# A two-layer transformer trunk on one core: loads of summed tiles issued six tiles back, two rests behind the shared results

## The chip, the core and the metric

The kernel runs on one core of a Trainium2 chip. What is measured is the device time of one execution in microseconds (us). Three runs of the kernel before gave 2206.82, 2209.60 and 2212.26 us; their median is 2209.6.

A core has five engines that run their own instruction queues and meet at semaphores: PE (TensorE, matrix products into the PSUM banks), DVE (VectorE, elementwise work), ACT (ScalarE), POOL (GpSimd, here only issuing transfers) and SP (SyncE, here only issuing transfers). Each engine takes its instructions strictly in order. Transfers from memory, whoever issues them, are carried by 16 DMA engines.

## The reference

`S` = 256 tokens of width 2048 go through two layers, everything in float32:

```python
for l in range(DEPTH):
    h = rms_norm(x, pre_mix_norm[l])
    m = hybrid_mixer(h, l, ...)          # w_in, two kinds of attention, w_o
    x = x + rms_norm(m, post_mix_norm[l])
    h = rms_norm(x, pre_ffn_norm[l])
    f = (silu(h @ w_gate[l]) * (h @ w_up[l])) @ w_down[l]
    x = x + rms_norm(f, post_ffn_norm[l])
```

`w_gate` and `w_up` are 2048 x 5632, `w_down` is 5632 x 2048. The weights are most of the 457 MB that are read in a run.

## The kernel before

**Weights as a stream.** The weights lie in memory as one list of tiles in the order of use, `weights_in_turn`: tile i has 128 partitions of 2 x 512 numbers, 512 KB, and holds two blocks of 128 rows by 512 columns of one matrix. In the texts "raw162" is tile 162 of this stream.

**Split products.** For float32 accuracy each operand is split into a high part and a rest. For a weight tile, ACT copies `raw` to `hi` (a shorter format, L271) and DVE subtracts it, `lo = raw - hi` (L273, called the "rest"). PE then makes three products per block: high by high, high by rest, rest by high (`product`, L976 to L978). The buffers: 4 of `raw`, 6 of `hi`, 6 of `lo`. A `raw` buffer is free for the next load when its rest has been made.

**Seven products in place of eight.** In the feed-forward part some pairs of tiles (`sevens`) are used in a form that needs seven block products where eight would stand, in the manner of Strassen and Winograd. Such a pair is a G tile (the gate tile, or the first of two down tiles) and a T tile (its partner). T is loaded by SP (L223), and then a second transfer, issued by POOL, adds one half of the G tile's data from memory onto its first half (`accum_op=ALU.add`, L224). `mixed_weights` makes the other sums of the pair on DVE and splits them: `hi`/`lo` from T, `Th`/`Tl` from further sums. In chunk 0 of the gate and up products two of eight pairs are such pairs, in chunk 1 three, in the others four; in each half of the down product seven of 22.

**Shared results.** Four of the seven products land in four PSUM banks of their own (`p1`, `p6`, `p7`, `q5`), over all pairs of a chunk. After the chunk's last such pair, `shared_part` turns them into four tiles `w[0]` to `w[3]`: one copy on ACT, four sums on DVE, at L1014 to L1017. They are then added to the chunk's other four banks (L1152, L1154). The banks are used in turn by the next chunk, which cannot begin in a bank before it has been read.

**The order of work.** `weights(i, ahead)` calls `feed(i + 1 + LOOKAHEAD)`, and that calls `fetch`, so loads and splits of a tile are written four tiles before its products. `fetch` also loads T tiles up to `EARLY` = 4 tiles beyond: it writes the load of a T before the load of the tile it is looking at. A scheduler then sets each engine's order, moving loads ahead as buffers come free. There are three G buffers and four T buffers in the gate and up products, and three of each in the down product. Behind the front, for instance, SP's order in layer 0 is raw161, T169, G164, T171, G168, T173, raw162; DVE's is L1014, a rest, L1015, L1016, L1017, a rest.

**The stages of a layer.** The input projection and attention, the output projection, then the gate and up products in 11 chunks of 512 columns (layer 0 from about 405 us, layer 1 from about 1500 us), then the down product in two halves, with a tail of three pairs at the end of the second.

Of the kernel before, what the change touches and what calls it, by code (L numbers as in the profile page):

```python
# [2 lines left out]

# [6 lines left out]
F32 = mybir.dt.float32  # L10
# [3 lines left out]
ALU = mybir.AluOpType  # L14
# [7 lines left out]
NT = S // P  # L22
# [27 lines left out]
WARM = 13  # L50
LEVEL = 232
EARLY = 4
X_BACK = 12


# [4 lines left out]
def gate_sevens(c):  # L60

    return (FIRST_SEVEN, NEXT_SEVEN)[c] if c < 2 else SEVEN
# [89 lines left out]
def kernel(  # L152
# [15 lines left out]
    nc = tc.nc  # L168
# [14 lines left out]
    def four_banks(odd, names):  # L183
        makers = (bank, bank, bank, last_bank) if odd else (acc_bank,) * 4
        return [make(n) for make, n in zip(makers, names)]
# [3 lines left out]
    stream = [weights_in_turn[i].rearrange("p (k n) -> p k n", k=2) for i in range(len(order))]  # L189

    ready = {}
    raws, loads = [], []
    fed = [0]

    def fetch(upto):
        while len(raws) < min(upto, len(stream)):
            i = len(raws)
            for j in range(i, min(i + EARLY + 1, mix_raw[3])):
                if j in sevens and j not in sums:
                    summed(j)  # L200
            if i in sevens:
                raws.append(sums[i])
                continue
            if i + 1 in sevens:
                g = mix_raw[0].tile([P, 2, CW], F32, tag="G", bufs=mix_raw[1], name=f"G{i}")
                loads.append(nc.sync.dma_start(g, stream[i]))
                raws.append(g)
                continue
            if i in own or i + 1 in own:
                raw = mix_pool[0].tile([P, 2, CW], F32, tag="v", bufs=2, name=f"V{i}")  # L210
            elif i in plain or i + 1 in plain:
                raw = mix_pool[0].tile([P, 2, CW], F32, tag="GU", bufs=4, name=f"GU{i}")
            else:
                raw = wpool.tile([P, 2, CW], F32, tag="raw", bufs=4, name=f"raw{i}")
            loads.append(nc.sync.dma_start(raw, stream[i]))
            raws.append(raw)

    sums = {}

    def summed(i):  # L220

        sums[i] = mix_raw[0].tile([P, 2, CW], F32, tag="T", bufs=mix_raw[2], name=f"T{i}")
        loads.append(nc.sync.dma_start(sums[i], stream[i]))  # L223
        nc.gpsimd.dma_start(sums[i][:, 0, :], stream[i - 1][:, 0, :], accum_op=ALU.add)  # L224

    mix_pool = [None]
# [34 lines left out]
    def feed(upto):  # L261
        fetch(upto)
        while fed[0] < min(upto, len(stream)):
            i = fed[0]
            raw = raws[i]
            if i in sevens or i in plain or i in own:
                ready[i] = mixed_weights(i)
                fed[0] += 1
                continue
            hi = wpool.tile([P, 2, CW], F32R, tag="hi", bufs=6, name=f"hi{i}")  # L270
            nc.scalar.activation(hi, raw, AF.Copy)  # L271
            lo = wpool.tile([P, 2, CW], F32R, tag="lo", bufs=6, name=f"lo{i}")
            rest = nc.vector.tensor_tensor(out=lo, in0=raw, in1=hi.bitcast(F32), op=ALU.subtract)  # L273
            ready[i] = (hi, lo)
            fed[0] += 1
            rests.append(rest)

    rests = []

    def after_rests():  # L280

        return tc.issue_after(rests[-1].ins)
# [5 lines left out]
    def weights(i, ahead):  # L288
        feed(i + 1 + ahead)
        return ready[i]  # L290
# [175 lines left out]
    def start(gen, n=1):  # L466
        running.append([clock[0] + n, gen])
# [542 lines left out]
    def shared_part(extra, w):  # L1010

        p1, p6, p7, q5 = extra
        nc.scalar.copy(w[0], p1)
        nc.vector.tensor_tensor(out=w[1], in0=p6, in1=w[0], op=ALU.subtract)  # L1014
        nc.vector.tensor_tensor(out=w[2], in0=p7, in1=w[1], op=ALU.add)  # L1015
        nc.vector.tensor_tensor(out=w[1], in0=q5, in1=w[1], op=ALU.add)  # L1016
        nc.vector.tensor_tensor(out=w[3], in0=q5, in1=w[2], op=ALU.add)  # L1017

    def shared_sign(t, col):
        return ALU.subtract if (t, col) == (1, 0) else ALU.add  # L1020

    xT = None
    for l in range(L):
# [11 lines left out]
        mg = {}  # L1035
# [16 lines left out]
        for kp in LATE_O:  # L1052
            i, j = (plan[l]["o"][c, kp] for c in (2, 3))
# [4 lines left out]
            if kp == O_SEVEN[0]:  # L1058
                extra = four_banks(False, [f"{q}_o{l}" for q in ("p1", "p6", "p7", "q5")])
            hi, lo = weights(i, LOOKAHEAD)  # L1060
# [64 lines left out]
        for c in range(FF // CW):  # L1125
            banks = four_banks(1 - c % 2, [f"c{q}_{l}_{c}" for q in ("11", "12", "21", "22")])
            mine = gate_sevens(c)
            order = FIRST_ORDER if c == 0 else tuple(range(KT // 2))
            if c == 0:
                for t in range(NT):  # L1130
                    for kp in order[:2]:
                        eight(banks, c, kp, (t,), kp == order[0], False)
                order = order[2:]
            extra = None
            for n, kp in enumerate(order):
                if (c, n) in FORM_AT:
                    with after_rests():
                        pair_sums(FORM_AT[c, n])
                if kp not in mine:
                    eight(banks, c, kp, range(NT), kp == 0, kp == order[-1])  # L1140
                    continue
                if kp == mine[0]:
                    extra = four_banks(c % 2, [f"{q}_{l}_{c}" for q in ("p1", "p6", "p7", "q5")])
                seven(banks, extra, c, kp, kp == mine[0], kp == mine[-1])
                if kp == mine[-1]:
                    w = [pool.tile([P, CW], F32, tag="t2", name=f"w{j}_{l}_{c}") for j in range(4)]
                    shared_part(extra, w)
            at = pool.tile([P, 4, S], F32, tag="act", bufs=FF // CW, name=f"act{l}_{c}")
            act.append(at)
            sg = [w[0], w[2]]  # L1150
            for t, u in ((0, w[1]), (1, w[3])):
                nc.vector.tensor_tensor(out=sg[t], in0=banks[2 * t], in1=sg[t], op=shared_sign(t, 0))  # L1152
                nc.scalar.activation(sg[t], sg[t], AF.Silu, scale=rs[t][:, 0:1])
                nc.vector.tensor_tensor(out=u, in0=banks[2 * t + 1], in1=u, op=ALU.add)  # L1154
                nc.vector.scalar_tensor_tensor(out=sg[t], in0=u, scalar=rs[t][:, 0:1], in1=sg[t], op0=ALU.mult, op1=ALU.mult)

            def flip(sg=sg, at=at, c=c):
                for t in range(NT):
                    pb = (acc_bank if c % 2 else bank)(f"actT_ps{l}_{c}_{t}")
                    for j in range(4):  # L1160
                        nc.tensor.transpose(pb[:, j * P : (j + 1) * P], sg[t][:, j * P : (j + 1) * P], ident)
                    nc.scalar.copy(at[:, :, t * P : (t + 1) * P], pb.rearrange("p (k q) -> p k q", k=4))
                    yield 1

            start(flip(), DEFER_ACT)
# [7 lines left out]
        mg = {}  # L1173
        ssm = [small.tile([P, 4], F32, tag="ssm", name=f"ssm_d{l}_{t}") for t in range(NT)]
        nkp = FF // P // 2
        for half in range(2):
# [48 lines left out]
            for kp in range(nkp - tail):  # L1225
                if half == 1 and kp == X_BACK:
                    back = [pool.tile([P, 4, S], F32, tag="act", bufs=FF // CW, name=f"xd{l}_{n}") for n in range(4)]
                    back = [b.rearrange("p k n -> p (k n)") for b in back]
                    xs[:] = [back[:2], back[2:]]
                    with in_turn():  # L1230
                        for t, h in ((0, 0), (0, 1), (1, 0), (1, 1)):
                            load_x(t, h, away[-1])
                if kp not in mine:
                    down(kp, range(NT))
                    continue
                if kp == mine[0]:
                    extra = four_banks(1 - half, [f"{q}_d{l}_{half}" for q in ("p1", "p6", "p7", "q5")])
                down_seven(kp)
                if kp == mine[-1]:
                    for t in range(NT):  # L1240
                        mg[t, half] = dn.tile([P, 2, CW], F32, tag="qk", bufs=4, name=f"mg_d{l}_{t}_{half}")
                    shared_part(extra, [mg[t, half][:, j, :] for t in range(NT) for j in range(2)])
                    if open_sums[0]:
                        for c in cc:
                            nc.vector.tensor_tensor(out=accs[c, 1], in0=accs[c, 1], in1=mg[1, half][:, c % 2, :], op=shared_sign(1, c % 2))
# [5 lines left out]
            for t in range(NT):  # L1251
# [4 lines left out]
                for c in cc:  # L1256
                    for kp in range(nkp - tail, nkp):
# [3 lines left out]
                        hi, lo = weights(plan[l]["down"][c, kp], LOOKAHEAD)  # L1261
# [67 lines left out]
```

## Time and profile before

| | |
|---|---|
| median of three runs | 2209.6 us (2206.82 to 2212.26) |
| the profiled execution | 2204.91 us |
| its span in the profile | 2203.2 us |
| clock granted to PE | 0.999 |
| PE / DVE / ACT / POOL busy | 2180.6 / 1902.2 / 1371.9 / 140.2 us |
| DMA, mean | 212 GB/s |
| loads from SP of ordinary, T and G tiles | 522, 110 and 110, of 512 KB each |
| sums onto T tiles, issued by POOL | 110, of 256 KB each |

How to read it: a busy row gives an engine's busy time, its share of the span and its instructions. PEld is the loading of weights into PE's array, which overlaps the products. A row of a timeline gives the start, the duration, the engine, the line and operation, and in brackets how long the engine stood idle before and what released it. A row such as "lo<-raw,hi" names what is written and what is read. SPq stands for SP's queue, and its rows are the issuing of transfers. PE's products overlap: each shows some 0.39 us, while the next starts earlier.

### The profile page before, as it was taken

Reading aid. Unit: us, or ns where it says so; the run is one execution under the profiler, and the core shown is the slowest. Engines: PE = TensorE matmul, PEld = TensorE weight load, DVE = VectorE, ACT = ScalarE, POOL = GpSimd, SP = SyncE. Lnnn points to the kernel's source line nnn. Section 1 sums busy time; section 2 is a strip of 40 time slices with the busy share of each in tenths; the row PEclk is TensorE's granted clock in tenths of the full one; section 3 lists DMA queues with packets and bytes.
Section 4 is the critical chain, followed back from the end, with each engine's and each line's share of the span. In section 5 each row is a group of like instructions: output and inputs, shape, how many; then the busy total and the mean of one; then the engine's idle time right before and its main releaser. Section 6 shows DMA issues by size and latency. Waiting matters only on the chain.

```text
span 2203.2 us, 28510 instructions
## 1 busy us (share of the span) xinstructions
PE 2180.6 (99%) x9991; PEld 1788.1 (81%) x9991; DVE 1902.2 (86%) x2609; ACT 1371.9 (62%) x2052; POOL 140.2 (6%) x186
## 2 busy tenths in 40 slices
PE   9999999999999999999999999999999999999998
PEld 7788888778888888888878888887788888888886
DVE  7888658899999999989888886579999999999897
ACT  7566665656656656666665666657566556566664
POOL 1200000000000000000011000000000000000000
PEclk9999999999999999999999999999999999999999
DMA  8654555776776675767465545658677677767683
GB/s 313 204 178 153 191 189 169 251 246 215 224 248 215 211 255 183 247 214 260 153 230 191 171 162 183 192 171 267 212 224 237 222 220 238 231 212 233 205 261 102
DMA packets 138512, 467.27 MB, mean 212 GB/s; under 512 B 15872, under 2 KB 16640, under 8 KB 137856
## 3 DMA queue, kind: packets, MB, share of 16 engines
q1 hardware_dynamic: 120656, 430.30, 56.5%
q0 software_dynamic: 15840, 28.84, 7.8%
q10 hardware_dynamic: 1872, 6.31, 0.8%
q8 instruction: 78, 1.28, 0.2%
q14 instruction: 66, 0.54, 0.1%
HBM read 457.00 MB, written 8.39 MB: 211 GB/s over the span
## 4 chain that ended last, share of the span: by engine, by line
PE 84%; DVE 9%; issue 2%; DMA 2%; ACT 2%; SPq 0%; DVEq 0%; ACTq 0%
PE c L976 8%; PE c L978 8%; PE c L977 8%; PE in L976 6%; PE in L978 6%; PE in L977 6%; PE dn L1212 4%; PE dn L1210 4%; PE dn L1209 4%; DVE lo L273 2%; PE p L977 2%; PE p L976 2%; PE p L978 2%; PE o L492 2%; PE o L493 2%
## 5 line engine op out<-in xcount | busy, mean ns | idle before, releaser
L273 DVE TENSOR_TENSOR lo<-raw,hi 128x1024 fp32r<-128x1024 f32 x522 | 627.5, 1220 | 122.6 <-ACT hi L271 121.4
L271 ACT ACTIVATE hi<-raw 128x1024 fp32r<-128x1024 f32 x522 | 541.1, 1053 | 234.8 <-DMA raw<-in_weights_in_turn_dram 71.7
L976 PE MATMUL c<-hi,xF 128*128 128x512 f32 x834 | 328.2, 396 | 3.5 <-DVE w L1017 1.6
L977 PE MATMUL c<-lo,xF 128*128 128x512 f32 x834 | 325.2, 390 | 0.5 <-DVE lo L273 0.5
L978 PE MATMUL c<-hi,xF 128*128 128x512 f32 x834 | 324.6, 390 | 0.0
L224 POOL DMA_DIRECT2D T<-in_weights_in_turn_dram x110 | 95.8, 874 | 1685.5 <-DMA T<-in_weights_in_turn_dram 596.5
L976 PEld LDWEIGHTS c<-hi,xF 128*128 128x128 f32 x834 | 156.3, 188 | 38.7 <-ACT hi L271 3.8
L977 PEld LDWEIGHTS c<-lo,xF 128*128 128x128 f32 x834 | 156.7, 188 | 33.5 <-DVE lo L273 2.7
L978 PEld LDWEIGHTS c<-hi,xF 128*128 128x128 f32 x834 | 156.6, 188 | 32.8
L1209 PE MATMUL dn<-hi,jh 128*128 128x512 f32 x432 | 168.3, 389 | 0.0
L1210 PE MATMUL dn<-lo,jh 128*128 128x512 f32 x432 | 168.1, 389 | 0.0
L273 DVE TENSOR_TENSOR lo<-G,hi 128x1024 fp32r<-128x1024 f32 x110 | 134.0, 1219 | 33.8 <-ACT hi L271 33.7
L245 ACT ACTIVATE Th<-G 128x1024 fp32r<-128x1024 f32 x110 | 116.0, 1055 | 40.2 <-DVE G L253 38.3
L246 DVE TENSOR_TENSOR Tl<-G,Th 128x1024 fp32r<-128x1024 f32 x110 | 134.0, 1218 | 5.3 <-ACT Th L245 5.3
L245 ACT ACTIVATE hi<-T 128x1024 fp32r<-128x1024 f32 x110 | 115.4, 1049 | 36.1 <-PE c L978 26.5
L246 DVE TENSOR_TENSOR lo<-T,hi 128x1024 fp32r<-128x1024 f32 x110 | 134.0, 1218 | 2.7 <-ACT hi L245 2.7
L253 DVE TENSOR_TENSOR G<-G,T 128x1024 f32<-128x1024 f32 x110 | 134.2, 1220 | 1.9
L1212 PE MATMUL dn<-hi,jl 128*128 128x512 f32 x432 | 133.0, 389 | 0.0
L245 ACT ACTIVATE Th<-T 128x512 fp32r<-128x512 f32 x110 | 68.9, 627 | 101.7 <-DVE T L252 85.5
L976 PE MATMUL in<-hi,xT 128*128 128x512 f32 x328 | 131.6, 402 | 0.0
L976 PE MATMUL in<-hi,xI 128*128 128x512 f32 x328 | 130.6, 401 | 0.0
L977 PE MATMUL in<-lo,xI 128*128 128x512 f32 x328 | 128.2, 391 | 1.5 <-DVE lo L273 1.5
(448 smaller groups left out, 4733.6 us busy)
## 6 DMA issues: line engine op xcount, KB each, us to landing
raw<-in_weights_in_turn_dram SPq DMA_DIRECT2D x522, 512.0 KB, 4.7
T<-in_weights_in_turn_dram SPq DMA_DIRECT2D x110, 512.0 KB, 4.5
G<-in_weights_in_turn_dram SPq DMA_DIRECT2D x110, 512.0 KB, 5.3
T<-in_weights_in_turn_dram POOLq DMA_DIRECT2D x110, 256.0 KB, 6.9
GU<-in_weights_in_turn_dram SPq DMA_DIRECT2D x32, 512.0 KB, 4.6
V<-in_weights_in_turn_dram SPq DMA_DIRECT2D x8, 512.0 KB, 3.9
away_ffn<-x ACTq DMA_DIRECT2D x8, 512.0 KB, 4.1
xd<-away_ffn SPq DMA_DIRECT2D x8, 512.0 KB, 8.1
```

The costliest lines, as they stand in the source:

```text
L224: nc.gpsimd.dma_start(sums[i][:, 0, :], stream[i - 1][:, 0, :], accum_op=ALU.add)
L245: nc.scalar.activation(h, w, AF.Copy)
L246: nc.vector.tensor_tensor(out=l, in0=w, in1=h.bitcast(F32), op=ALU.subtract)
L253: nc.vector.tensor_tensor(out=g, in0=g, in1=t2.unsqueeze(1).to_broadcast([P, 2, CW]), op=ALU.add)
L271: nc.scalar.activation(hi, raw, AF.Copy)
L273: rest = nc.vector.tensor_tensor(out=lo, in0=raw, in1=hi.bitcast(F32), op=ALU.subtract)
L976: nc.tensor.matmul(a, sh, hi, start=first, stop=False, skip_group_check=open_sums[0])
L977: nc.tensor.matmul(a, sh, lo, start=False, stop=False, skip_group_check=open_sums[0])
L978: nc.tensor.matmul(a, sl, hi, start=False, stop=last, skip_group_check=open_sums[0])
L1209: nc.tensor.matmul(accs[c, t], sh, hi[:, kk, :], start=first, stop=False, skip_group_check=open_sums[0])
L1210: nc.tensor.matmul(accs[c, t], sh, lo[:, kk, :], start=False, stop=False, skip_group_check=open_sums[0])
L1212: nc.tensor.matmul(accs[c, t], sl, hi[:, kk, :], start=False, stop=last, skip_group_check=open_sums[0])
```

## The change

Two edits, neither of which adds or removes an instruction.

The first makes SP issue a G or T load only behind the last ordinary load (raw, GU or V) whose place in the stream is at least `LEAD` = 6 before the tile's own. `tc.issue_after` puts the instructions in its block behind the named one in their queue's order; the wait for a buffer remains as it was.

The second returns the last instruction of `shared_part` and keeps it in `held` with a count of 2. The next two rests that `feed` makes (not those in `mixed_weights`) are put behind this instruction in DVE's order. It is used in the gate and up products and in the down product.

```diff
+LEAD = 6
...
             if i + 1 in sevens:
                 g = mix_raw[0].tile([P, 2, CW], F32, tag="G", bufs=mix_raw[1], name=f"G{i}")
-                loads.append(nc.sync.dma_start(g, stream[i]))
+                with not_ahead(i):
+                    loads.append(nc.sync.dma_start(g, stream[i]))
...
             loads.append(nc.sync.dma_start(raw, stream[i]))
             raws.append(raw)
+            usual.append((i, loads[-1]))
+
+    usual = []
+
+    def not_ahead(i):
+
+        return tc.issue_after(next(load.ins for j, load in reversed(usual) if j <= i - LEAD))
...
     def summed(i):
...
-        loads.append(nc.sync.dma_start(sums[i], stream[i]))
+        with not_ahead(i):
+            loads.append(nc.sync.dma_start(sums[i], stream[i]))
         nc.gpsimd.dma_start(sums[i][:, 0, :], stream[i - 1][:, 0, :], accum_op=ALU.add)
...
-            rest = nc.vector.tensor_tensor(out=lo, in0=raw, in1=hi.bitcast(F32), op=ALU.subtract)
+            with behind():
+                rest = nc.vector.tensor_tensor(out=lo, in0=raw, in1=hi.bitcast(F32), op=ALU.subtract)
...
+    held = [None, 0]
+
+    def behind():
+
+        if held[1] == 0:
+            return nullcontext()
+        held[1] -= 1
+        return tc.issue_after(held[0].ins)
...
-        nc.vector.tensor_tensor(out=w[3], in0=q5, in1=w[2], op=ALU.add)
+        return nc.vector.tensor_tensor(out=w[3], in0=q5, in1=w[2], op=ALU.add)
...
-                    shared_part(extra, w)
+                    held[:] = shared_part(extra, w), 2
...
-                    shared_part(extra, [mg[t, half][:, j, :] for t in range(NT) for j in range(2)])
+                    held[:] = shared_part(extra, [mg[t, half][:, j, :] for t in range(NT) for j in range(2)]), 2
```

After it, SP's order at the start of layer 0's feed-forward part is raw145, raw146, G152, raw147, T153, raw148, raw149, T155, G154, raw150, raw151, T157, G156, where before it was raw145, T153, T155, G152, T157, G154, raw146, T165, raw147 to raw150, G156, raw151. In a chunk further on it is raw191, T197, raw192, G188, raw193, G196, raw194, G200, raw195, T201, raw198, T203, raw199, T205, G202; before, T197 stood behind raw192, and T201 and T203 ahead of raw194. On DVE the four sums of `shared_part` follow each other, with the two rests behind them. On PE and ACT the order changes in about 50 places each, all by a few instructions; on POOL it does not.

More of the change, by code (lines that the diff above doesn't have):

```diff
@@ L1 @@
 import math
-from contextlib import ExitStack
+from contextlib import ExitStack, nullcontext
 import concourse.bass as bass
```

## The prediction

> **What bounds the kernel now.** I read the page first, then a table of stretches, then what TensorE waits for, then the timelines around its gaps.
>
> ```profile
> span 2203.2 us, 28510 instructions
> PE 2180.6 (99%) x9991; PEld 1788.1 (81%) x9991; DVE 1902.2 (86%) x2609; ACT 1371.9 (62%) x2052; POOL 140.2 (6%) x186
> ...
> T<-in_weights_in_turn_dram SPq DMA_DIRECT2D x110, 512.0 KB, 4.5
> ...
> T<-in_weights_in_turn_dram POOLq DMA_DIRECT2D x110, 256.0 KB, 6.9
> ```
>
> TensorE (PE) is busy for all but 22.6 of 2203.2 us, so only its gaps can be won. T and G tiles exist only in the two feed-forward parts (about 405 to 1090 and 1500 to 2150 us), so I look for the gaps there. The columns are PE, PEld, DVE, ACT, POOL, then clock, DMA share and GB/s.
>
> ```profile
> 450.00:500.00 50.00, 48.50 (x219) 38.87 (x217) 45.30 (x60) 28.76 (x35) 2.60 (x3) 1.00 0.65 205
> 500.00:550.00 50.00, 49.05 (x221) 39.94 (x219) 46.86 (x51) 31.10 (x36) 4.34 (x5) 1.00 0.76 237
> 550.00:800.00 250.00, 250.00 (x1127) 207.03 (x1126) 233.59 (x252) 151.69 (x175) 20.91 (x24) 1.00 0.71 227
> ...
> 1600.00:1650.00 50.00, 49.06 (x220) 40.26 (x220) 47.37 (x52) 30.24 (x35) 4.35 (x5) 1.00 0.71 218
> 1650.00:1900.00 250.00, 250.00 (x1128) 207.08 (x1127) 233.63 (x252) 152.07 (x174) 20.86 (x24) 1.00 0.72 227
> ```
>
> From 550 and from 1650 us on there is no gap at all: nothing is to be won there, and DVE, busy 93%, has little to lose. The gaps stand in the first chunks of each layer's gate and up products: 1.50 + 0.95 us in layer 0. The largest pair, on PE, DVE, ACT and SP:
>
> ```profile
> 488.90 0.39 PE L978 MATMUL c<-hi,xF 128*128 128x512 f32 x1
> 489.74 0.50 PE L976 MATMUL c<-hi,xF 128*128 128x512 f32 x1 [0.45 <-DVE w L1015]
> ...
> 490.32 0.40 PE L978 MATMUL c<-hi,xF 128*128 128x512 f32 x1
> 491.53 0.50 PE L976 MATMUL c<-hi,xF 128*128 128x512 f32 x1 [0.81 <-DVE w L1017]
> ```
>
> ```profile
> 483.47 0.68 DVE L1014 TENSOR_TENSOR w<-p,w 128x512 f32<-128x512 f32 x1
> 487.86 1.23 DVE L273 TENSOR_TENSOR lo<-raw,hi 128x1024 fp32r<-128x1024 f32 x1 [3.71 <-ACT hi L271]
> 489.00 0.68 DVE L1015 TENSOR_TENSOR w<-p,w 128x512 f32<-128x512 f32 x1
> ...
> 490.80 0.68 DVE L1017 TENSOR_TENSOR w<-q,w 128x512 f32<-128x512 f32 x1
> ```
>
> ```profile
> 486.77 1.06 ACT L271 ACTIVATE hi<-raw 128x1024 fp32r<-128x1024 f32 x1 [7.66 <-DMA raw<-in_weights_in_turn_dram]
> ```
>
> ```profile
> 474.42 0.33 SPq L223 DMA_DIRECT2D T<-in_weights_in_turn_dram  x1
> 476.17 0.33 SPq L206 DMA_DIRECT2D G<-in_weights_in_turn_dram  x1
> 477.91 0.33 SPq L223 DMA_DIRECT2D T<-in_weights_in_turn_dram  x1
> 479.04 0.33 SPq L215 DMA_DIRECT2D raw<-in_weights_in_turn_dram  x1
> ```
>
> Read from the bottom: an ordinary tile (raw162 in the order of instructions) is issued at 479.04 behind a T, a G and a T, and its split on ACT starts only at 486.77, 7.7 us later. Its rest on DVE stands in program order between L1014 and L1015, so DVE idles 3.71 us with the shared results half done; PE needs the PSUM banks that L1015 and L1017 free, and stops twice. Its starts are 0.227 us apart in dense work (0.39 long, pipelined). Here 488.90 to 489.74 is 0.61 too long, the two steps after it 0.13, the step to 491.53 0.98: a gap costs what the profile shows as idle and about 0.28 us of refilling.
>
> **The change part by part.** No instruction is added or removed on any engine; POOL's order is the same. Two things move.
>
> *The loads.* Each T and G goes behind the ordinary load six places up. At the place above the order becomes raw161, G164, raw162, G168, raw163, T169, raw166, T171, raw167, T173: of T171, G168 and T173, none is any longer in front of raw162. What a load costs the 16 DMA engines comes from a full stretch, 421 to 437 us, and the one behind it, 437 to 456:
>
> ```profile
> DMA  9999999999999999999999999999987948966589
> GB/s 225 312 369 369 302 312 282 271 292 358 384 394 435 389 440 389 451 430 410 410 379 420 399 440 399 440 369 348 389 348 200 143 97 154 179 113 87 108 123 164
> ...
> q1 hardware_dynamic: 1171, 4.27, 68.6%
> q0 software_dynamic: 398, 0.71, 28.7%
> ```
>
> ```profile
> q1 hardware_dynamic: 1288, 4.69, 67.1%
> q0 software_dynamic: 379, 0.68, 19.7%
> ```
>
> At some 410 GB/s, 524,288 bytes take 1.28 us. Three loads less in front of raw162 are 3.8 us: it lands 3.8 us earlier at best, 0 at worst (if all loads in flight share alike). I take the upper end, because the 7.7 us stand so far above the 4.5 us that the page gives as the median of a load of this size.
>
> *The rests.* L1014 to L1017 now run back to back and the next two rests behind them, so a late tile can no longer hold the banks. At 483.47 the shared results would be done by about 486, ahead of PE's need at 489.13 (488.90 + 0.227). This part alone removes the pair, whatever the loads do: 0.45 + 0.81 + 2 x 0.28 = 1.8 us. Layer 1 has the same place, and three smaller gaps of the two layers go with late tiles:
>
> ```profile
> 1587.67 0.50 PE L976 MATMUL c<-hi,xF 128*128 128x512 f32 x1 [0.83 <-DVE w L1017]
> ```
>
> ```profile
> 474.94 0.50 PE L976 MATMUL p<-Th,sh 128*128 128x512 f32 x1 [0.20 <-ACT Th L245]
> ```
>
> ```profile
> 1554.17 0.51 PE L977 MATMUL c<-lo,xF 128*128 128x512 f32 x1 [0.51 <-DVE lo L273]
> ```
>
> ```profile
> 1571.65 0.50 PE L976 MATMUL p<-Th,sh 128*128 128x512 f32 x1 [0.18 <-ACT Th L245]
> ```
>
> The sum. (A) Banks: 1.8 in layer 0, 0.83 + 0.28 = 1.1 in layer 1: 2.9 us, in full. (B) Late splits ahead of them: in 450 to 500 us what is left of 1.50 after the pair is 0.24, in two gaps, so 0.8 us with refilling; in layer 1 0.51 + 0.18 + 0.56 = 1.25: 2.05 us. They end with the tiles in earlier; bounds 0 and 2.05, taken in full, since the 3.8 us above are many times the lateness. (C) The windows 500 to 550 and 1600 to 1650 hold 0.95 and 0.94 us, two gaps each, in which PE waits for the last Tl of a seven:
>
> ```profile
> PE p L977 <- DVE Tl L246: 2.4, 6, 0.5
> ```
>
> With refilling 3.0 us. DVE regains its 3.71, less one rest (1.13) that now goes ahead of these Tl, which covers the 0.5. But the T tiles of the second gap are now issued last of all. I take the first gap of each layer, 0.82 x 2 = 1.6, and leave the second; bounds 0 and 3.0. Sum 2.9 + 2.05 + 1.6 = 6.6 us; the ceiling is 2.9 + 2.05 + 3.0 = 8.0.
>
> What I cost at nothing is the held pair in the 16 or so later chunks where there is no gap. There DVE and ACT show:
>
> ```profile
> 566.30 2.35 DVE L273 TENSOR_TENSOR lo<-raw,hi 128x1024 fp32r<-128x1024 f32 x2
> 568.57 0.68 DVE L1014 TENSOR_TENSOR w<-p,w 128x512 f32<-128x512 f32 x1
> ...
> 572.85 0.69 DVE L1152 TENSOR_TENSOR w<-c,w 128x512 f32<-128x512 f32 x1 [0.51 <-PE c L978]
> ...
> 587.14 1.23 DVE L273 TENSOR_TENSOR lo<-G,hi 128x1024 fp32r<-128x1024 f32 x1 [2.06 <-ACT hi L271]
> ```
>
> ```profile
> 579.70 1.06 ACT L271 ACTIVATE hi<-raw 128x1024 fp32r<-128x1024 f32 x1 [2.81 <-issue]
> ```
>
> After the change one of the two rests at 566.30 and one that stood behind L1015 go behind L1017. DVE then may stand at L1014 from 567.44 to 568.57 at the latest, and all six are done by about 573.4 instead of 572.34: at most 0.55 us past the 572.85 at which L1152 has its operand, against 2.06 us in which DVE idles at 587.14 anyway. Without that cover it would be 0.55 x 16 = 9 us. The rests also free the buffers of the next raw loads, some 3 us later than before; ACT's next ordinary split is at 579.70, after 2.81 us in which nothing kept it waiting, so these loads have 11 us from 568.6, where a load needs 4.5 and the shift takes 3: covered by over 3 us. Behind the moved T loads POOL's accumulates start later by as much: 4.5 us for the load and 6.9 for the sum are to be had inside six tiles.
>
> The page "Perfetto Trace Analysis" of the Trainium skill, section Identifying the Most-Contended Engine, says that the busy share of matmuls is not a good measure of the headroom and that of the weight loads is. By that rule the stretch 550 to 800 (207.03 of 250, 82.8%) is what dense work shows here, and 450 to 550 (78.81 of 100) falls short by 4.8 us, where the six gaps with their refilling give 2.45 + 6 x 0.28 = 4.1. The sum would by it be about a sixth larger, some 7.7 us; I keep the gaps, which stand row by row.
>
> **The rivals.**
>
> (1) *All gaps go*, the second Tl gap too: 7.2 to 8.0 us, some 2202. For it: DVE has 2.6 us in hand where 0.5 is missing. Against: T173 is issued later than before.
>
> (2) *The prefetch moves into a crowded stretch.* Before, two T, a G, a T and a G are issued in 421 to 437 us, ahead of raw146, which is issued when its buffer comes free:
>
> ```profile
> 436.91 0.33 SPq L215 DMA_DIRECT2D raw<-in_weights_in_turn_dram  x1
> ```
>
> After, all five stand behind it, and only one T moves out of the next stretch. Four loads of 1.28 us are 5.1 us; 437 to 456 is 87% full, which leaves 0.13 x 19 = 2.4. So tiles for the first chunk come up to 2.7 us late, and PE waits before 460 us, in both layers: 6.6 - 2 x 2.7 = 1.2 us are left, 2208. Against: the T and G were issued far ahead of their use, and ordinary tiles go first now.
>
> (3) *The held rests starve the later chunks* (slower). One mechanism: the raw loads behind the held rests are issued 3 us later in every chunk; where one then takes the 7.7 us that raw162 took, it arrives at 568.6 + 3.5 + 7.7 = 579.8 and ACT, and behind it DVE's Tl, runs late. It decides from the point at which DVE loses more than its 2.06 us per chunk. At 0.5 to 1 us past it in 16 chunks it costs 8 to 16 us: net 1.5 to 9.5 slower, some 2215. For it: DVE is 93% busy, and the pair goes behind a wait. Against: DMA is busy only 71% there.
>
> (4) *A T sum comes late* (slower): a T issued behind raw149 needs 4.5 + 6.9 us and more in a full stretch; ACT then stands at its split with every later split behind it. Two to five us in each layer's first chunks: around 2211 to 2213.
>
> That the change does nothing is a rival only for the loads:
>
> ```profile
> SPq L215 <- DVE lo L273: 1146.0, 462, 16.9
> ```
>
> Ordinary loads are issued when a rest frees a buffer, whatever stands beside them. Then (A) is left: 2.9 us, 2206.7. I count it with (2).
>
> **How the numbers follow.** The forecast's sum against the profiled execution is 2203.2 - 6.6 = 2196.6 us of span. That execution took 2204.91, 4.7 below the median of the three runs, 2209.6; from the median the forecast is 2203.0. Chances: forecast 0.46, (1) 0.25, (2) with the loads doing nothing 0.10, (3) 0.13, (4) 0.06. What a measurement of this kernel can tell from no change is 0.3%, 6.6 us, and the forecast lies on that line: half of it counts as faster, half as the same. Faster 0.23 + 0.25 = 0.48; same 0.23 + 0.10 = 0.33; slower 0.13 + 0.06 = 0.19. The range goes from (1) with the scatter of three runs (2.8 us below their median), 2199, to the middle of (3), 2215. The forecast's own is 2200 to 2207.
>
> **What would show it.** Right: no wait of PE for L1015 or L1017 near 489 and 1587 us, DVE's four shared results back to back, raw162 landing within 5 us, PE in 450 to 500 above 49.7, and 250.00 of 250 still in the later windows. (C) is wrong if PE still waits for Tl at about 500. (2) shows as waits of PE or ACT before 460 and 1560 us. (3) shows as PE below 250 in 550 to 800, and as ACT waiting for DMA there; (4) as ACT waiting for T from POOL's queue. The forecast is wrong as a whole if the gaps near 489 go and the same time comes back further down.

## The result, and the profile after

Five runs of the changed kernel gave a median of 2199.37 us (2199.20 to 2203.41), five of the kernel before on the same chip 2208.44. The ratio is 0.996, 95% interval 0.9949 to 0.9972: faster by 6 to 11 us. The forecast, a gain of 6.6 us, lies inside this interval, near its lower end. The time itself, 2199.4 us, lies below the forecast's own 2200 to 2207 and at the lower edge of the whole range (2199 to 2215), the edge that rival (1), all gaps go, had set.

The profiled execution of the changed kernel took 2203.41 us, with a span of 2201.7; it is the slowest of the five. So the two spans, 2203.2 and 2201.7, do not show the gain, and the profile has to be read stretch by stretch. First the table of stretches (span, then busy time and instruction count of PE, PEld, DVE, ACT, POOL, then clock, DMA share, GB/s):

```profile
450.00:500.00 50.00, 50.00 (x229) 40.96 (x228) 48.66 (x63) 29.65 (x36) 5.21 (x6) 1.00 0.81 268
500.00:550.00 50.00, 50.00 (x225) 40.97 (x224) 47.64 (x51) 32.13 (x37) 4.35 (x5) 1.00 0.77 243
550.00:800.00 250.00, 250.00 (x1128) 207.02 (x1127) 233.42 (x253) 151.29 (x175) 20.93 (x24) 1.00 0.71 227
1600.00:1650.00 50.00, 50.00 (x225) 41.09 (x224) 47.84 (x53) 29.78 (x35) 4.36 (x5) 1.00 0.70 217
1650.00:1900.00 250.00, 250.00 (x1128) 206.87 (x1127) 233.42 (x252) 151.11 (x175) 20.90 (x24) 1.00 0.71 227
```

Where PE stood idle for 1.50, 0.95 and 0.94 us, it is idle for nothing, and the later stretches are full as before. In this one execution time is lost elsewhere, as the waits of PE show (in total, times, longest):

```profile
PE in L996 <- DVE lo L284: 4.2, 3, 3.1
PE p L995 <- ACT Th L255: 1.4, 1, 1.4
PE xT_ps L427 <- DVE xd L557: 1.3, 1, 1.3
...
PE p L996 <- DVE Tl L256: 0.5, 2, 0.2
```

Both waits for shared results (w) of the gate and up products are gone, and the waits for Tl fall from 2.4 us in six to 0.5 in two. Against that stand one wait of 3.1 us in the input projection of layer 1 (1.2 before) and one of 1.4 us for Th at 433.60 us; the wait for xd was there before (1.4). The first differs from one execution to the next, and the second occurs without either edit too (both below).

### The profile page after: what moved, and what is told of

It reads as the page before. It is cut to its first block, busy times and chain, and to the rows that moved or that the text cites. A ratio compares the mean times of both kernels' runs of the same rounds, so it can differ in the third digit from the quotient of the medians.

```text
span 2201.7 us, 28554 instructions
## 1 busy us (share of the span) xinstructions
PE 2180.2 (99%) x9991; PEld 1789.3 (81%) x9991; DVE 1904.0 (86%) x2609; ACT 1371.4 (62%) x2052; POOL 140.4 (6%) x186
## 3 DMA queue, kind: packets, MB, share of 16 engines
q8 instruction: 78, 1.28, 0.2%
## 4 chain that ended last, share of the span: by engine, by line
PE 90%; DVE 5%; ACT 2%; DMA 1%; issue 1%; SPq 0%; DVEq 0%; ACTq 0%
PE c L996 10%; PE c L997 10%; PE c L995 10%; PE in L997 6%; PE in L996 6%; PE in L995 6%; PE dn L1231 4%; PE dn L1229 4%; PE dn L1228 4%; PE p L996 3%; PE p L995 3%; PE p L997 3%; PE o L511 2%; PE o L512 2%; PE o L513 2%; DVE lo L284 2%
## 5 line engine op out<-in xcount | busy, mean ns | idle before, releaser
L996 PE MATMUL in<-lo,xT 128*128 128x512 f32 x328 | 128.1, 391 | 0.8 <-DVE lo L284 0.8
```

The source lines that it names most:

```text
L996: nc.tensor.matmul(a, sh, lo, start=False, stop=False, skip_group_check=open_sums[0])
```

## The experiments

Times are medians, each against runs of the kernel before on the same chip.

| kernel | us | ratio to before, 95% |
|---|---|---|
| changed kernel, again | 2199.19 | 0.9944 to 0.9972 |
| loads alone | 2199.71 | 0.9948 to 0.9973 |
| loads alone, first three chunks | 2199.74 | 0.9951 to 0.9976 |
| loads alone, from the fourth chunk on | 2208.80 | 0.9995 to 1.0013 |
| held rests alone | 2204.82 | 0.9976 to 0.9993 |
| both edits off | 2208.67 | 0.9991 to 1.0009 |
| LEAD = 10 | 2201.37 | 0.9959 to 0.9984 |
| LEAD = 2 | 2203.08 | 0.9971 to 0.9990 |
| held rests made twice | 2216.57 | 1.0026 to 1.0053 |
| first sums on DVE | 2202.69 | 0.9969 to 0.9987 |
| first sums on DVE, written early | 2199.85 | 0.9954 to 0.9978 |

**Each part alone.** The loads alone have both counts at zero:

```diff
-                    held[:] = shared_part(extra, w), 2
+                    held[:] = shared_part(extra, w), 0
```

> The change with its loads alone; the rests stay where they were, between L1014 and L1015. My theory: raw162 lands within 5 us of its issue (7.7 before), so the rest in front of L1015 is made in time and nearly all gaps of the first chunks go, also those for the banks: 5 to 6.6 us faster than before, PE in 450 to 500 us above 49.5 of 50. Rival, the loads do nothing because rests set their issue: raw162 takes 7 us and more again, the gaps near 489 and 1587 us stay, time as before within 1 us. Rival, crowded stretch: gaps appear before 460 and 1560 us, 0 to 3 us faster.

The held rests alone let `not_ahead` do nothing:

```diff
-        return tc.issue_after(next(load.ins for j, load in reversed(usual) if j <= i - LEAD))
+        return nullcontext()
```

> The change with its held rests alone; the loads keep the order of before. My theory: PE's two waits for L1015 and L1017 go (2.9 us), while raw162 still takes 7 to 8 us, DVE idles some 3 us behind its shared results, and PE's waits for Tl at about 504, 526, 1600 and 1622 us stay (3 us): 2 to 3 us faster than before. Rival, the held rests are the whole of the gain: 6 us and more faster, Tl waits gone as well. Rival, held rests starve later chunks: PE below 250.0 of 250 in 550 to 800 us, slower than before.

The loads alone are 8.7 us faster than before, more than I expected, though PE was busy for only 49.15 us in 450 to 500, less than I expected: a wait for Th of 0.85 us stands at 476.85. The held rests alone give 3.6 us (1.5 to 5.3 by the interval); together the two edits give 9.2 us, which the runs can't tell from the loads alone. So the loads make the gain, and the rests save a part of the same time. The place near 489 us shows why. With the held rests alone (SP, then ACT, then DVE):

```profile
482.54 0.33 SPq L217 DMA_DIRECT2D raw<-in_weights_in_turn_dram  x1
```

```profile
490.06 1.06 ACT L281 ACTIVATE hi<-raw 128x1024 fp32r<-128x1024 f32 x1 [7.64 <-PE c L997]
```

```profile
486.97 0.69 DVE L1033 TENSOR_TENSOR w<-p,w 128x512 f32<-128x512 f32 x1
...
489.10 0.68 DVE L1036 TENSOR_TENSOR w<-q,w 128x512 f32<-128x512 f32 x1
491.15 1.22 DVE L284 TENSOR_TENSOR lo<-raw,hi 128x1024 fp32r<-128x1024 f32 x1 [1.38 <-ACT hi L281]
```

The tile is as late as before, 7.5 us from issue to split (the row names PE; the load landed at 489.95), but the four shared results no longer wait for it, and PE does not wait for them. The lateness shows further on: PE waits for Th and Tl at 506 and 508 us.

```profile
506.13 0.73 PE L995 MATMUL p<-Th,sh 128*128 128x512 f32 x2 [0.91 <-ACT Th L255]
507.92 0.50 PE L996 MATMUL p<-Tl,sh 128*128 128x512 f32 x1 [0.59 <-DVE Tl L256]
```

In the second profile of the changed kernel, with the loads moved, the same tile is split 3.4 us after its issue, and no wait follows before 550 us:

```profile
480.38 0.33 SPq L217 DMA_DIRECT2D raw<-in_weights_in_turn_dram  x1
```

```profile
483.80 1.06 ACT L281 ACTIVATE hi<-raw 128x1024 fp32r<-128x1024 f32 x1 [3.85 <-DMA raw<-in_weights_in_turn_dram]
```

DVE makes the four shared results there one behind the other, and has them by 487.3 us:

```profile
484.46 0.69 DVE L1033 TENSOR_TENSOR w<-p,w 128x512 f32<-128x512 f32 x1
485.25 0.69 DVE L1034 TENSOR_TENSOR w<-p,w 128x512 f32<-128x512 f32 x1
485.98 0.69 DVE L1035 TENSOR_TENSOR w<-q,w 128x512 f32<-128x512 f32 x1
486.59 0.68 DVE L1036 TENSOR_TENSOR w<-q,w 128x512 f32<-128x512 f32 x1
487.19 1.22 DVE L284 TENSOR_TENSOR lo<-raw,hi 128x1024 fp32r<-128x1024 f32 x1
```

**The changed kernel and the kernel before, once more.**

> The changed kernel once more, for a second profile. My theory: PE's waits at 433.60 (1.41 us, for Th) and 1122.65 (3.14 us, for a rest in the input projection of layer 1) in the first profile of after are one execution's late transfers, since no moved load precedes either in its stage; here they are smaller by 1 us or more at one of the two places, and the span is near 2197.5. If they are made by the change, both are there again with the same lengths and the span is near 2201.7. Time 0.9945 to 0.998 of before.

> The kernel before once more, for a second profile. My theory: the gaps of the first chunks of gate and up (457 to 527 and 1550 to 1623 us) are there again, 5 to 8 us with refilling, and what else differs from the first profile lies at the starts of the stages. If executions differ by more than 2 us inside the changed stretch, part of the measured gain is that scatter and not the mechanism.

The changed kernel took 2199.19 us (span 2197.5). Its wait in the input projection of layer 1 was 0.94 us in place of 3.14: an execution's own. The wait for Th at 433 us came again, 1.50 us. The kernel before, at 2206.31 us, had gaps in the same chunks that cost about as much, if not all at the same products: at the banks 0.81 us alone, without the 0.45, and 0.76 us for a rest at 459.11. It had no wait at 433 us. Since every kernel with an edit had one so far, this asked for a control.

**Both edits off.** Both of the edits above at once; every engine's order is that of before.

> The changed program with both edits switched off (no load is put behind another, no rest is held): on every engine it has the order of the kernel before. Control for the wait of 1.4 to 2.2 us at about 433 us (PE for Th, the first pair of layer 0) that all profiles of kernels with an edit show and neither profile of before. My theory: its cause is an order that the edits change, so it is absent here, and the time is that of before within 0.1%. Rival: it is scatter of the placement of the program, and shows here too. If the ratio is off 1 by more than 0.1%, part of the measured 0.4% is not the change.

The ratio is 1.000 (0.9991 to 1.0009), so at most 2 us of the gain could come from the build. The wait at 433 us is there:

```profile
432.28 0.72 PE L995 MATMUL p<-Th,sh 128*128 128x512 f32 x2 [1.46 <-ACT Th L255]
...
492.23 0.50 PE L995 MATMUL c<-hi,xF 128*128 128x512 f32 x1 [1.38 <-DVE w L1034]
494.02 0.79 PE L995 MATMUL c<-hi,xF 128*128 128x512 f32 x1 [0.83 <-DVE w L1036]
```

My theory of it falls: no edit is needed for it. In this execution the first bank gap is 1.38 us; the two profiles of before have 0.45 and none there. How much the order of before loses therefore differs from profile to profile. That is best seen between the first transposes (`actT_ps`) of successive chunks, which mark the same place in each: 192 or 193 products of PE stand in the first step and 189 or 190 in the next, before as after. From the kernel before, from both edits off, and from the changed kernel's second profile, the first four of layer 0:

```profile
452.67 0.60 PE L1161 MATMUL actT_ps<-ident,w 128*128 128x128 f32 x4
497.81 0.60 PE L1161 MATMUL actT_ps<-ident,w 128*128 128x128 f32 x4
541.09 0.60 PE L1161 MATMUL actT_ps<-ident,w 128*128 128x128 f32 x4
582.86 0.60 PE L1161 MATMUL actT_ps<-ident,w 128*128 128x128 f32 x4
```

```profile
453.31 0.60 PE L1180 MATMUL actT_ps<-ident,w 128*128 128x128 f32 x4
501.72 0.60 PE L1180 MATMUL actT_ps<-ident,w 128*128 128x128 f32 x4
543.75 0.60 PE L1180 MATMUL actT_ps<-ident,w 128*128 128x128 f32 x4
585.48 0.60 PE L1180 MATMUL actT_ps<-ident,w 128*128 128x128 f32 x4
```

```profile
454.01 0.60 PE L1180 MATMUL actT_ps<-ident,w 128*128 128x128 f32 x4
496.86 0.60 PE L1180 MATMUL actT_ps<-ident,w 128*128 128x128 f32 x4
538.89 0.60 PE L1180 MATMUL actT_ps<-ident,w 128*128 128x128 f32 x4
580.66 0.60 PE L1180 MATMUL actT_ps<-ident,w 128*128 128x128 f32 x4
```

By differences the first step takes 45.14, 48.41 and 42.85 us, the second 43.28, 42.03 and 42.03, the third 41.77, 41.73 and 41.77. The change saves time in the first two steps, and nothing from the third on. Four profiles have the order of before in these chunks (the fourth is that of a kernel of the next experiment), two that of the changed kernel:

| profile | layer 0, two steps | layer 1, two steps | sum, us |
|---|---|---|---|
| before | 45.14 + 43.28 | 45.31 + 43.32 | 177.05 |
| before, once more | 45.62 + 43.29 | 45.45 + 43.29 | 177.65 |
| both edits off | 48.41 + 42.03 | 45.84 + 43.29 | 179.57 |
| loads alone, from the fourth chunk on | 46.22 + 43.32 | 45.28 + 43.30 | 178.12 |
| changed | 42.81 + 42.01 | 42.87 + 42.01 | 169.70 |
| changed, again | 42.85 + 42.03 | 43.31 + 42.00 | 170.19 |

The order of before is 6.9 to 9.9 us longer here, so these two steps of each layer hold the measured gain of 9 us.

Not all of the 48.41 us is waiting. Behind the gap at 494.02 us PE's products start 0.43 us apart instead of 0.227, and the granted clock (third column from the right) is below 1:

```profile
490.00:495.00 5.00, 2.79 (x9) 1.69 (x8) 4.65 (x6) 2.44 (x4) 0.00 (x0) 0.87 0.91 300
495.00:500.00 5.00, 5.00 (x19) 4.00 (x18) 5.00 (x8) 3.59 (x5) 0.00 (x0) 0.79 0.32 114
```

Seven products in a row take 3.13 us there, and 1.70 us behind the same gap of 0.83 us in the fourth profile, where the clock stays at 1.00: 1.4 us that no wait shows. The first profile of the changed kernel has the same behind its wait of 3.14 us: the clock is 0.74 from 1120 to 1125 us, and eight products take 3.39 us where the second profile needs 1.98. So of the 4.2 us between its two spans, 2.2 are the longer wait and 1.4 the lower clock behind it.

**Which chunks.** The loads alone again, in two halves, by the place in the stream:

```diff
     def not_ahead(i):
+        if i % 392 >= 176:
+            return nullcontext()
```

and the other with `<` in place of `>=`.

> The loads alone (no rest is held), put behind the tile six up only in chunks 0 to 2 of the gate and up products of each layer (stream places below 176 of a layer's 392); PE, DVE and ACT then have the order of the loads alone. My theory: the whole gain is made there, since later chunks have no gap: the time of the loads alone within 1.5 us (2198.5 to 2201), PE without waits between 450 and 550 us and between 1560 and 1650 us but one or two short ones. Rival, the later chunks carry part of it: 2203 to 2206.

> The other half: the loads put behind only from place 176 on, later chunks and the down product; PE, DVE and ACT have the order of before. My theory: no gain, 2206 to 2209, with the gaps of before at 457 to 527 and 1550 to 1623 us. Rival, part of the gain is here: 2202 to 2205.

The first three chunks of each layer carry all of it, the rest nothing; the second half shows the bank and Tl gaps of before (0.16 and 0.83 us at the banks), and a wait of 1.59 us for Th at 433.33. PE's own stretches had said so: where it has no gap, an earlier load wins nothing.

**Other leads.**

> LEAD = 10 in place of 6: at the start of each layer's gate and up products T153, T155, G152 and G154 go ahead of raw146 again, and T169, G164, T171 and G168 ahead of raw162 (before: also T173); the rests are held. My theory: raw162 lands 5 to 7 us after its issue, the gaps for the banks are gone by the held rests, and the waits for Tl at about 504 and 1600 us come back in part: 1 to 4 us slower than the changed kernel. Rival, the exact lead is of no weight: the time of the changed kernel within 1 us.

> LEAD = 2 in place of 6: each T and G four tiles (some 10 us of PE's time) later at most than in the changed kernel; in a later chunk it moves a T by about one tile. My theory: T sums have some 6 us and more in hand, so the time is that of the changed kernel within 2 us (2198 to 2202), and PE stays at 250.0 of 250 in 550 to 800 us. Rival, T sums come late: ACT waits for T from POOL's queue, PE has gaps in many chunks, 8 us and more slower than the changed kernel.

LEAD = 10 loses some 2 us of the gain, as expected; the interval overlaps that of the changed kernel, but the waits for Th and Tl are back at 502.62 and 504.40 us (1.02 and 0.59). LEAD = 2 did not do as I expected. It loses nearly 4 us, not 2 at most, though by single waits in the first chunks and not in many. One is at 476.64 us (1.11), the other in layer 1:

```profile
1571.34 0.49 PE L996 MATMUL p<-Tl,sh 128*128 128x512 f32 x1 [1.33 <-DVE Tl L256]
```

Twelve us ahead of it ACT stands before the split of a T tile:

```profile
1559.55 1.06 ACT L255 ACTIVATE hi<-T 128x1024 fp32r<-128x1024 f32 x1 [1.54 <-DVE G L263]
```

The row names DVE, whose sum is of another tile; the tile that ACT splits is T547, whose sum by POOL landed at 1559.07, 14.7 us after its load was issued. DVE, which needs the split, idles 1.87 us up to 1561.16 and then works without a pause up to the Tl that PE waits for. In the first chunks, then, T tiles have less in hand than the 6 us I gave them, and a late T sum is the price on the other side of the lead.

**The cover of the held rests.** Each held rest is made twice:

```diff
+            again = 2 if held[1] else 1
             with behind():
-                rest = nc.vector.tensor_tensor(...)
+                for _ in range(again):
+                    rest = nc.vector.tensor_tensor(...)
```

> The changed kernel with each of the two held rests made twice (51 more DVE instructions of 1.22 us, some 2.3 us in each chunk, behind the shared results). It measures the cover of the held rests. My theory: in a later chunk DVE has 2.06 us idle, of which the change takes up to 0.55, so 2.3 us more are short by about 0.8 us in each of some 20 chunks: 6 to 20 us slower than the changed kernel, PE below 249 of 250 in 550 to 800 us. Rival, the cover is larger than the idle time shows, since DVE can run behind: within 2 us of the changed kernel.

It cost 17 us, within the expected range, but not where I expected it. From 550 to 800 us:

```profile
550.00:800.00 250.00, 250.00 (x1120) 204.71 (x1119) 244.93 (x265) 150.45 (x174) 20.90 (x24) 1.00 0.72 229
```

DVE takes 11.5 us more than the 233.4 of the changed kernel, nearly all out of its idle time. PE shows no idle time at all, where I had expected less than 249 us of work, yet it did 1120 products in place of some 1128: a gap shorter than 0.16 us does not show, as a product is drawn 0.39 us long and the next starts 0.227 later. A later chunk became 0.0 to 0.45 us longer, less than my 0.8. More was lost at the ends of the stretch, in the first chunks and where the last chunk's results have to be ready for the down product:

```profile
874.24 0.66 PE L1182 MATMUL actT_ps<-ident,w 128*128 128x128 f32 x4 [1.37 <-DVE w L1176]
```

Behind this wait, too, the granted clock is lower, 0.66 from 875 to 880 us, and so it is from 435 to 440 us, behind a wait of 1.78 us for Th. So the cover of the change's own shift, at most 0.55 us, holds in the later chunks; it is thinnest at the turns.

**A version without the wait at 433 us.** POOL's transfers for the first two T tiles of each layer are left out, and DVE adds G's half in their place:

```diff
+    by_hand = {l * 392 + i for l in range(L) for i in (139, 141)}
...
-        nc.gpsimd.dma_start(sums[i][:, 0, :], stream[i - 1][:, 0, :], accum_op=ALU.add)
+        if i not in by_hand:
+            nc.gpsimd.dma_start(sums[i][:, 0, :], stream[i - 1][:, 0, :], accum_op=ALU.add)
...
-        if i in plain or i in own:
+        if i in plain or i in own or i in by_hand:
```

> The changed kernel, with the sums onto the first two T tiles of each layer (T139, T141, T531, T533) made by DVE (four more sums of 128 x 512, 0.68 us each) in place of POOL's transfers. These land some 10 us after their issue, among four ordinary loads, and PE's wait of 1.4 us for Th at 433 us is for one of them. My theory: that wait goes, DVE has idle time there for its sums: 1 to 2.5 us faster than the changed kernel (2197 to 2198.5). Rival, PE waits for DVE in its place (Tl or Th of the same pair): the time of the changed kernel within 1 us, or slower.

The wait at 433 went and another took its place, at 437.60 (1.17 us, hi of T141) and, new, at 1534.36 (1.18): DVE made T141's sum only at 435.64, behind the whole first pair. A wait of 1.23 us for Th came at 478.25 too. The rival was right; it was 3.5 us slower than the changed kernel. So both sums were written at once, ahead of the first pair's splits:

```diff
+        if i + 2 in by_hand and i in by_hand:
+            fetch(i + 2)
+            for j in (i, i + 2):
+                nc.vector.tensor_tensor(out=sums[j][:, 0, :], in0=raws[j - 1][:, 0, :], in1=sums[j][:, 0, :], op=ALU.add)
```

> As the kernel with the first two sums of each layer on DVE, but both sums are written at once, ahead of the first pair's splits, so that the second pair's split on ACT (hi of T141) no longer stands behind a sum that DVE makes late. My theory: PE's waits at 433 us (1.4 us, Th) and at 437 and 1534 us (1.2 us, hi of T141) are both gone, and the time is 1 to 3 us below the changed kernel (2196.5 to 2198.5). Rival: a split of the first pair (Th139), which now stands behind one more ordinary split on ACT, comes late instead: PE waits for Th at about 433 us by 0.5 us or more, and the time is that of the changed kernel or slower.

All three waits are gone. Between 419 and 550 us and between 1514 and 1650 PE has one wait of 0.1 us or more each, 0.46 us for Th at 475.06 and 0.40 us for a rest at 1553.88. The time did not follow, 2199.85 us, that of the changed kernel within the scatter. In the profiled execution a wait of 2.40 us in layer 1's input projection (0.94 and 3.14 in the profiles of the changed kernel), with a clock of 0.66 in 1120 to 1125 us behind it, took more than was won. I have no version that is shown to beat the change.

## Why the prediction was right, and where it was off

**The bound and the place.** Right. PE's gaps in the first chunks were where the time was to be won, and the two halves of the loads show that nothing was won elsewhere.

**The chain at 489 us.** Right in each link: the late tile, the idle DVE, the banks. Three loads less in front were to bring the tile in up to 3.8 us earlier; it came 4.3 us earlier (3.4 us from issue to split, 7.7 before). That is 0.5 us more than the upper end, and the runs do not show what makes it up.

**(A), the banks.** The gap went, but I gave it to the held rests as theirs whatever the loads do. Each part alone removes it. The rests' own gain, 3.6 us with a wide interval, agrees with the 2.9 of the sum; on top of the loads they are worth nothing that the runs can tell.

**(B), late splits.** Right: with the tiles in earlier the waits for a rest and for Th ahead of the banks go, from 450 us on in the first profile after.

**(C), the Tl gaps.** This is the term that was mis-sized. I took the first gap of each layer and left the second, on the ground that T173 is issued later. Both went, and from 500 to 550 and from 1600 to 1650 us PE is full. The second step of each layer holds these gaps alone: between the two first profiles it became 1.27 and 1.31 us shorter, 2.6 us where the sum has 1.6. That is rival (1), the likelier reading of the result.

**The sum.** The first steps hold (A) and (B). They became 2.3 and 2.4 us shorter between the same two profiles, 4.8 us where the sum has 4.95. All ten gaps, with 4.9 us of idle time, cost 6.9 to 7.4 us, so refilling took some 0.2 to 0.25 us each and not 0.28. That the sum of 6.6 us lies so near these 6.9 to 7.4 owes something to luck, since two gaps too few and a price too high went opposite ways. The rest of the measured 9 us is likely that of the execution that the gaps were taken from. The other three profiles with the order of before lose 0.6, 1.1 and 2.5 us more in the same steps; of the 2.5 us, 1.4 are the lower clock behind the bank gaps, for which the prediction has no term. The profile of before also took less time than most, 2204.91 us, where the medians of before are 2207.4 to 2208.4.

**The crowded stretch (2).** The DMA engines do fall idle before raw146 is issued (0.03 and 0.00 busy in 430 to 435 and 435 to 440 us, 0.94 and 0.92 before) and are then full; PE nonetheless has no wait between the Tl wait at 440.9 us and 550 us. The moved tiles were needed later than the ordinary ones that now go first. Its companion, that the loads do nothing, is refuted by the loads alone.

**The held rests in later chunks (3)** cost nothing: PE is full there, and the chunk time of 41.77 us is the same to a hundredth before and after. **T sums late (4)** did not occur at LEAD = 6; at LEAD = 2 one does.

**The busy share of the weight loads.** By it the estimate was 7.7 us against 6.6 by the gaps. From 450 to 550 us that share rose from 78.81 to 81.93 of 100, so 3.1 of the 4.0 up to the 82.8 of dense work were won, which is 3.8 us of time at 82.8%. In layer 0 it agrees with the measured steps (3.6 us between the same two profiles).

## What to carry to other kernels

In a queue of loads, what stands in front of a load decides when it lands (here raw162 took 7.4 and 7.6 us from issue to landing behind a T, a G and a T, and 3.3 and 3.4 us ahead of them): put the load that is needed next ahead of prefetches that have slack, but not so far ahead that these come late in turn. An instruction that may wait for a late operand should not stand in the middle of a chain that frees a resource others wait for. Gaps taken from one profile are one draw: take further profiles, of the same order of instructions, before sizing a gain by them, and look at the granted clock behind a gap too, since the wait may not be all that it costs.

## What was not expected of the hardware

The same order of instructions ran in two ways in the first pairs of layer 0. The kernel before, twice, had no wait at 433 us; with both edits off, and with the loads moved only from the fourth chunk on, it had one of 1.46 and 1.59 us. What differs is when the first sums by POOL's transfers land: the sum onto T139 took 5.7 and 6.3 us from its issue in the two profiles of before, 8.6 and 8.5 us in the other two. This goes with the moment of its issue. In the profiles without the wait POOL issued it 1.28 and 1.73 us ahead of the first of the ordinary loads that SP issues next, in the other two 0.51 us. The edits do not set that: both profiles of the changed kernel had 0.6 us and the wait, LEAD = 10, with both edits on, had 1.74 us, a landing in 6.6 us and no wait. What sets the moment is open, and so is whether it changes from execution to execution or from build to build, since the kernels that were profiled twice did the same both times.

The granted clock fell behind some of PE's waits, for some 3 us: to a mean of 0.66 in 435 to 440 us behind a wait of 2.16 us (the held rests alone, at 434.67), and as told above behind waits of 1.38 and 0.83 us close together, of 3.14, 2.40, 1.78 and 1.37 us. It did not behind 1.41, 1.50 and 1.59 us at 433 us, nor behind 2.63 us at 1124.07 (first sums on DVE). The length of the wait alone does not decide it, and what does was not looked into.
